# Attention in a decoder trunk: plain float32 matmuls for scores and for the products with V, in place of three products of split parts

## The chip, the cores and the metric

The kernel runs on one core of one Trainium2 chip. The metric is the device time of one execution in microseconds (us). Engines are named as the profile names them: PE is TensorE's matmul stream, PEld its weight loads, DVE is VectorE, ACT is ScalarE, SP issues the DMAs.

## What is computed

A decoder trunk of two layers on 256 tokens of width 1024, all in float32: a gated short convolution with a feed-forward block (ConvGLU), then attention with a feed-forward block, then a norm. With 256 tokens there is one block of keys, so the block selection falls away and the attention is plain causal attention of 16 heads of 64 columns, with a bias that depends on the distance. The part that the change touches, cut to what matters:

```python
sc = einsum("hqd,hkd->hqk", q, k) * scale + bias      # per head; causal, else -1e30
p  = softmax(sc)
o  = einsum("hqk,hkd->hqd", p, v)                      # 16 heads x 64 columns
return o.reshape(256, 1024) @ w_o
```

## The kernel before

**Split operands.** Nearly every matmul is made of three: an operand x is split into `hi` (x written as fp32r) and `lo` (x minus hi), and `mm3` (lines 160 to 163) adds hi x hi, hi x lo and lo x hi in PSUM. Weights arrive by DMA as `rawB` (8 KB in a partition) or `rawS` (4 KB), ACT writes `hiB`/`hiS` (line 86), DVE writes `loB`/`loS` (line 92). For activations `split_act` (lines 362 to 366) does the same with the tiles `sh` and `sl`. A few small matmuls take plain float32 operands and no split: the sums of squares (line 320), a broadcast of a row (line 334) and the table of biases (line 351).

**Attention.** Two heads make a pair j, eight pairs in all. `heads` sets PE's order: `v_step` makes V in four blocks of 256 columns (0, 1, 2, and block 3 after the last pair), `qk_step(j)` makes Q and K of pair j transposed (48 matmuls of 256 columns into the bank `qb[j]`), and behind each comes `attend(i)`, which puts on PE the transposes of pair i-2, the scores of pair i-1 and the products with V of pair i-3, in this order, and behind them the work of ACT and DVE that feeds later calls. So scores of a pair stand alone behind `qk_step(1)` and, with transposes ahead of them, behind `qk_step(2)`; six calls have transposes, scores and products together (behind `qk_step(3)` to `qk_step(7)` and behind V's block 3); two more calls, between the steps of the output product `wo`, have products and no scores (the first has transposes ahead of them).

**Scores** (line 623): in a pair, head e lies on partitions 64e to 64e+63 of the tiles `qh` and `ql`, so a matmul of one head has 64 rows. The queries of the second 128 tokens see 256 keys, those of the first see 128. For each of the two chunks there are three products, and in each the two heads stand next to each other.

**Products with V** (`pv`, lines 668 to 674): for each head, `mm3` runs with all 128 columns of V that belong to the pair as weights (`vh`, `vl`) and with the transposed probabilities (`sh`, `sl`) as moving operand, 256 columns and then 128; of the 128 partitions of the result half is used (`o_out`, lines 679 and 682).

**Banks.** PSUM tiles come from two rings, `acc` (4 banks) and `up` (3). In the attention, `qb`, V's block 3 and the products take `up` banks.

Of the kernel before, what the change touches and what calls it, by code (L numbers as in the profile page):

```python
# [11 lines left out]
F32 = mybir.dt.float32  # L12
F32R = mybir.dt.float32r
I32 = mybir.dt.int32
AF = mybir.ActivationFunctionType
OP = mybir.AluOpType

S = 256
D = 1024
KT = D // 128  # L20
# [17 lines left out]
def f32(ap):  # L38
    return ap.bitcast(F32)
# [3 lines left out]
def yoco_kernel(ctx: ExitStack, tc: tile.TileContext, t: dict, out: bass.AP):  # L43
    nc = tc.nc
    V, A, G, PE = nc.vector, nc.scalar, nc.gpsimd, nc.tensor

    const = ctx.enter_context(tc.tile_pool(name="const", bufs=1))
    wpool = ctx.enter_context(tc.tile_pool(name="wpool", bufs=1))
    act = ctx.enter_context(tc.tile_pool(name="act", bufs=2))
    tmp = ctx.enter_context(tc.tile_pool(name="tmp", bufs=2))  # L50
# [46 lines left out]
    def hi(tag, part=0, parts=1):  # L97

        n = ptr[tag][0]
        if n < len(by_tag[tag]) and (by_tag[tag][n].prev is None or by_tag[tag][n].prev.used):  # L100
            by_tag[tag][n].split_hi(part, parts)
            ptr[tag][0] += part == parts - 1

    def lo(tag, part=0, parts=1):

        n = ptr[tag][1]
        if n < len(by_tag[tag]) and by_tag[tag][n].hi is not None:
            by_tag[tag][n].split_lo(part, parts)
            if part == parts - 1:
                ptr[tag][1] += 1  # L110
                if n + RAW_BUFS[tag] < len(by_tag[tag]):
                    by_tag[tag][n + RAW_BUFS[tag]].load()
# [47 lines left out]
    def mm3(o, wh, wl, xh, xl, start, stop):  # L160
        PE.matmul(o, wh, xh, start=start, stop=False, skip_group_check=True)  # L161
        PE.matmul(o, wh, xl, start=False, stop=False, skip_group_check=True)  # L162
        PE.matmul(o, wl, xh, start=False, stop=stop, skip_group_check=True)  # L163
# [74 lines left out]
    def shifted(pool, name, tag, rows, **kw):  # L238

        t = pool.tile([128, rows * S + 64], F32R, name=name, tag=tag, **kw)  # L240
        return t[:, 48:48 + rows * S].rearrange("p (k s) -> p k s", s=S)
# [14 lines left out]
    def parts_tiles(moved=False):  # L256
        return Rows("xh", moved), Rows("xl", moved)
# [58 lines left out]
    def rstd_cols(sq):  # L316

        ps = psum.tile([128, 512], F32, name="misc", bufs=1)
        for c in range(2):
            PE.matmul(ps[:, c:c + 1], sq[:, 2, c * 128:(c + 1) * 128], ones[:, 0:1],  # L320
                      start=(c == 0), stop=True, skip_group_check=True)
        w = tmp.tile([128, 8], F32, name="nw")
        ms, y, a = w[:, 0:2], w[:, 2:4], w[:, 4:6]
        V.tensor_scalar(ms, ps[:, 0:2], 1.0 / D, EPS, op0=OP.mult, op1=OP.add)
        rsqrt(ms, y, a)
        dg = tmp.tile([128, 2, 128], F32, name="dg", tag="bias")
        for c in range(2):
            V.tensor_scalar(dg[:, c, :], ident, y[:, c:c + 1], None, op0=OP.mult)
        return y, dg

    def rstd_rows(dg, scales=(1.0,), orders=(same,)):

        ps = psum.tile([128, 512], F32, name="misc", bufs=1)
        PE.matmul(ps[:, :S], ones, dg.rearrange("p c s -> p (c s)"), start=True, stop=True)
        r = act.tile([128, 2, S], F32, name="rr", bufs=1)
        for n, s in enumerate(scales):
            A.activation(r[:, n, :], orders[n](ps[:, :S]), AF.Copy, scale=s)
        return r
# [23 lines left out]
    def split_act(src, n):  # L362

        h, lw = (tmp.tile([128, 384 + 64], F32R, name="s" + x, tag="z" + x, bufs=4)[:, 16:16 + n]
                 for x in "hl")
        return (h, lw), lambda: A.activation(h, src, AF.Copy), lambda: V.tensor_sub(lw, src, f32(h))  # L366
# [28 lines left out]
    rr = None  # L395
# [39 lines left out]
    rr = rstd_rows(dg)  # L435
# [125 lines left out]
    hot = bias_load()  # L561
    xvh, xvl, sq = boundary(acc, xT, P_KVN, rev)
    xqh, xql = parts_tiles()
    vh = wpool.tile([128, 2, D], F32R, name="vh", tag="hiB2")
    vl = wpool.tile([128, 2, D], F32R, name="vl", tag="loB2")
    oh = None
    ol = shifted(act, "ol", "ol", KT, bufs=1)
    vb, qb, qs, sb, pr, pt, ps_, ob, bias = {}, {}, {}, {}, {}, {}, {}, {}, {}
    ycol = rr = None
# [15 lines left out]

    def v_out(n):
        cols = slice(n * 256, (n + 1) * 256)
        for c in range(2):
            A.activation(vh[:, c, cols], vb[n][:, c, :], AF.Identity, scale=ycol[:, c:c + 1])
        for c in range(2):  # L590
            V.scalar_tensor_tensor(vl[:, c, cols], vb[n][:, c, :], ycol[:, c:c + 1], f32(vh[:, c, cols]),
                                   op0=OP.mult, op1=OP.subtract)

    def qk_step(j, ks=range(KT)):
        u = WH["q", j]
# [7 lines left out]
        u.used = ks[-1] == KT - 1  # L603

    def qk_out(j):
        q = tmp.tile([128, 2, S], F32, name="u", bufs=2)
        V.tensor_mul(q, qb[j], rr)
        h = tmp.tile([128, 2, S], F32R, name="qh", tag="cv", bufs=2)
        lw = tmp.tile([128, 2, S], F32R, name="ql", tag="ql", bufs=2)
        A.activation(h, q, AF.Copy)  # L610
        qs[j] = h, lw
        return lambda: V.tensor_sub(lw, q, f32(h))

    def scores(j, bank):
        h, lw = qs[j]
        for e in range(2):
            sb[j, e] = bank()
        for c, cols in ((1, slice(0, 256)), (0, slice(256, 384))):
            tok, ks = slice(c * 128, (c + 1) * 128), slice(128 - c * 128, S)
            for n, (q, k) in enumerate(((h, h), (h, lw), (lw, h))):  # L620
                for e in range(2):
                    d = slice(e * 64, (e + 1) * 64)
                    PE.matmul(sb[j, e].rearrange("p a s -> p (a s)")[:, cols], q[d, 0, tok], k[d, 1, ks],  # L623
                              start=(c == 1 and n == 0), stop=(n == 2), skip_group_check=True)

    CHUNKS = ((0, slice(0, 256), slice(0, 256)), (1, slice(256, 384), slice(0, 128)))

# [22 lines left out]
    def transposes(j, bank):  # L650
        for e in range(2):
            pt[j, e] = bank()
            b = pt[j, e].rearrange("p a s -> p (a s)")
            p = pr[j, e]
            PE.transpose(b[:, 0:128], p[:, 256:384], ident)
            PE.transpose(b[:, 128:256], p[:, 128:256], ident)
            PE.transpose(b[:, 256:384], p[:, 0:128], ident)

    def pt_out(j):
        low = []  # L660
        for e in range(2):
            b = pt[j, e].rearrange("p a s -> p (a s)")[:, 0:384]
            ps_[j, e], make_hi, make_lo = split_act(b, 384)
            make_hi()
            low.append(make_lo)
        return lambda: [f() for f in low]

    def pv(j, bank):
        b = ob[j] = bank()
        f = slice(j * 128, (j + 1) * 128)  # L670
        for e in range(2):
            h, lw = ps_[j, e]
            mm3(b[:, e, :], vh[:, 1, f], vl[:, 1, f], h[:, 0:256], lw[:, 0:256], start=(e == 0), stop=False)
            mm3(b[:, e, 128:256], vh[:, 0, f], vl[:, 0, f], h[:, 256:384], lw[:, 256:384], start=False, stop=True)

    def o_out(j):
        for e in range(2):
            d = slice(e * 64, (e + 1) * 64)
            A.activation(oh[d, j, :], ob[j][d, e, :], AF.Copy)
        for e in range(2):  # L680
            d = slice(e * 64, (e + 1) * 64)
            V.tensor_sub(ol[d, j, :], ob[j][d, e, :], f32(oh[d, j, :]))

    class Held:

        used = False

    next(u for u in UP[1] if u.slot == 2).prev = Held
    low_q, low_p, fin = {}, {}, {}

    def attend(i, qk=True, s=True, tr=True, v=True, banks=(acc_bank, acc_bank, up_bank)):

        if tr and 0 <= i - 2 < KT:
            transposes(i - 2, banks[0])
        if s and 0 <= i - 1 < KT:
            scores(i - 1, banks[1])
        if v and 0 <= i - 3 < KT:
            pv(i - 3, banks[2])
        if qk:
            hi("B")  # L700
        if qk and i < KT:
            low_q[i] = qk_out(i)
        if tr and 0 <= i - 2 < KT:
            low_p[i - 2] = pt_out(i - 2)
        if s and 0 <= i - 1 < KT:
            fin[i - 1], inverse = softmax(i - 1)
        if qk:
            lo("B")
        if s and 0 <= i - 1 < KT:
            inverse()  # L710
        if tr and 0 <= i - 2 < KT:
            low_p[i - 2]()
        if qk and i < KT:
            low_q[i]()
        if v and 0 <= i - 3 < KT:
            o_out(i - 3)
        if s and 0 <= i - 1 < KT:
            fin[i - 1]()

    for kind, n in heads:  # L720
        if kind == "v":
            vb[n] = acc_bank() if n < 3 else up_bank()
            if n == 1:
                v_step(1, range(0, 4))
                bias_table(hot)
                ycol, dg = rstd_cols(sq)
                v_step(1, range(4, 8))
                oh = shifted(act, "oh", "oh", KT, bufs=1)
            elif n == 2:
                v_step(2, range(0, 2))  # L730
                rr = rstd_rows(dg, (-0.125, 1.0), (rev, same))
# [185 lines left out]
```

## Time and profile before

| | |
|---|---|
| median of 3 runs | 583.97 us (583.82 to 584.67) |
| profiled execution, its own time | 584.08 us |
| its span (first to last instruction) | 582.1 us |
| PE busy | 573.4 us (98%), 4745 matmuls |
| DVE busy, ACT busy | 460.9 us (79%), 359.7 us (62%) |
| chain of waits that ends last | PE 97% |

The profile is of one execution; 2.0 us of its time lie outside the span. A busy PE row means that matmuls were in flight; how fast they follow each other is read from the starts of neighbouring rows, since a matmul's own duration includes its way through the array.

### The profile page before, as it was taken

The page shows a single profiled execution, that of the slowest core. Times are in us where ns is not written, and L with a number is a line of the kernel's source. Part 1 is how long each engine was busy: PE and PEld are TensorE (multiplying, and loading weights), DVE is VectorE, ACT ScalarE, POOL GpSimd, SP SyncE. Part 2 cuts the span into 40 slices and gives each one's busy share as a digit, 9 for nine tenths or more (in the row PEclk, how much of TensorE's full clock was granted, in tenths as well). Part 3 has the DMA queues.
Part 4 walks back from the last instruction along what each step waited for, and adds up shares of the span by engine and source line. Part 5 has one row for each costly group of instructions (what it writes and reads, how often), then busy time and mean ns, then how long its engine had stood idle before and what let it go on. Part 6 is the DMA issues. An engine that isn't in the chain of part 4 may idle for free.

```text
span 582.1 us, 11537 instructions
## 1 busy us (share of the span) xinstructions
PE 573.4 (98%) x4745; PEld 558.4 (96%) x4745; DVE 460.9 (79%) x781; ACT 359.7 (62%) x570; POOL 3.6 (1%) x15
## 2 busy tenths in 40 slices
PE   8999999999999999999999999999999999999995
PEld 8999999999999999999999999999999999999994
DVE  5899769888778777877977887757997787777865
ACT  7765347566566555665758997748675566556443
POOL 0000000000000000000000000000000000000001
PEclk9999999999999999999999999999999999999999
DMA  8985673545554566544446564434655644553111
GB/s 290 404 285 195 214 256 114 212 147 217 217 187 166 191 217 213 173 167 175 147 171 220 181 243 165 145 110 146 218 180 218 216 169 169 207 216 117 65 37 73
DMA packets 24236, 108.51 MB, mean 186 GB/s; under 512 B 2759, under 2 KB 5496, under 8 KB 16248
## 3 DMA queue, kind: packets, MB, share of 16 engines
q1 hardware_dynamic: 23864, 107.46, 52.1%
q8 instruction: 37, 0.61, 0.4%
q10 hardware_dynamic: 320, 0.32, 0.2%
q14 instruction: 15, 0.12, 0.1%
HBM read 106.70 MB, written 1.07 MB: 185 GB/s over the span
## 4 chain that ended last, share of the span: by engine, by line
PE 97%; DMA 1%; ACT 1%; DVE 0%; issue 0%; SPq 0%; POOLq 0%; POOL 0%; DVEq 0%; ACTq 0%
PE up L161 20%; PE up L163 20%; PE up L162 20%; PE acc L161 7%; PE acc L163 7%; PE acc L162 6%; PE acc L189 3%; PE acc L188 3%; PE acc L187 3%; PE acc L623 1%; PE acc L579 1%; PE acc L581 1%; PE acc L582 1%; DMA xres<-xT 1%; PE up L582 0%; PE up L579 0%
## 5 line engine op out<-in xcount | busy, mean ns | idle before, releaser
L161 PE MATMUL up<-xh,hiB 128*128 128x256 f32 x944 | 263.2, 279 | 0.3 <-ACT hiB L86 0.3
L163 PE MATMUL up<-xh,loB 128*128 128x256 f32 x944 | 261.5, 277 | 0.2 <-DVE loB L92 0.2
L162 PE MATMUL up<-xl,hiB 128*128 128x256 f32 x944 | 261.7, 277 | 0.0
L161 PEld LDWEIGHTS up<-xh,hiB 128*128 128x128 f32 x944 | 177.5, 188 | 1.6 <-ACT hiB L86 0.6
L162 PEld LDWEIGHTS up<-xl,hiB 128*128 128x128 f32 x944 | 177.5, 188 | 0.8
L163 PEld LDWEIGHTS up<-xh,loB 128*128 128x128 f32 x944 | 177.4, 188 | 0.7 <-DVE loB L92 0.7
L92 DVE TENSOR_TENSOR loB<-rawB,hiB 128x2048 fp32r<-128x2048 f32 (+2 forms) x75 | 147.6, 1973 | 3.9 <-ACT hiB L86 3.9
L86 ACT ACTIVATE hiB<-rawB 128x2048 fp32r<-128x2048 f32 (+1 forms) x73 | 123.6, 1697 | 17.2 <-PE acc L582 6.0
L92 DVE TENSOR_TENSOR loS<-rawS,hiS 128x1024 fp32r<-128x1024 f32 (+2 forms) x73 | 83.7, 1148 | 13.8 <-ACT hiS L86 13.5
L498 ACT ACTIVATE cv<-u,pk 128x256 f32<-128x256 f32 x88 | 48.2, 595 | 72.8 <-DVE u L491 72.8
L369 DVE SCALAR_TENSOR_TENSOR cv<-u,pk,cv 128x255 f32<-128x255 f32 x192 | 81.4, 479 | 2.7 <-ACT cv L498 1.7
L86 ACT ACTIVATE hiS<-rawS 128x1024 fp32r<-128x1024 f32 (+1 forms) x71 | 71.6, 1010 | 9.7 <-PE acc L162 6.0
L491 DVE TENSOR_TENSOR u<-up,rr 128x512 f32<-128x512 f32 x44 | 30.3, 689 | 58.7 <-PE up L163 57.3
L161 PE MATMUL acc<-sh,hiS 128*128 128x256 f32 x240 | 66.3, 276 | 0.0
L163 PE MATMUL acc<-sh,loS 128*128 128x256 f32 x240 | 66.3, 276 | 0.0
L162 PE MATMUL acc<-sl,hiS 128*128 128x256 f32 x240 | 66.3, 276 | 0.0
L366 ACT ACTIVATE sh<-hid 128x256 fp32r<-128x256 f32 x52 | 21.7, 416 | 59.7 <-DVE hid L512 55.0
L163 PEld LDWEIGHTS acc<-sh,loS 128*128 128x128 f32 x240 | 45.1, 188 | 0.0
L161 PEld LDWEIGHTS acc<-sh,hiS 128*128 128x128 f32 x240 | 45.1, 188 | 0.0
L162 PEld LDWEIGHTS acc<-sl,hiS 128*128 128x128 f32 x240 | 45.1, 188 | 0.0
L189 PE MATMUL acc<-hiS,sl 128*128 128x512 f32 (+1 forms) x89 | 34.8, 391 | 0.0
L188 PE MATMUL acc<-loS,sh 128*128 128x512 f32 (+1 forms) x89 | 34.6, 389 | 0.0
(157 smaller groups left out, 756.9 us busy)
## 6 DMA issues: line engine op xcount, KB each, us to landing
rawB<-w_up SPq DMA_DIRECT2D x44, 1024.0 KB, 4.8
rawS<-w_dn SPq DMA_DIRECT2D x44, 512.0 KB, 3.4
rawB<-w_qk SPq DMA_DIRECT2D x8, 1024.0 KB, 4.9
rawB<-w_mc SPq DMA_DIRECT2D x6, 1024.0 KB, 7.7
rawS<-w_mo SPq DMA_DIRECT2D x8, 512.0 KB, 3.3
rawB<-w_v SPq DMA_DIRECT2D x4, 1024.0 KB, 4.8
rawS<-w_o SPq DMA_DIRECT2D x8, 512.0 KB, 3.5
rawS<-w_mb SPq DMA_DIRECT2D x7, 512.0 KB, 5.6
```

The costliest lines, as they stand in the source:

```text
L86: A.activation(self.hi[:, c], self.raw[:, c], AF.Copy)
L92: V.tensor_sub(self.lo[:, c], self.raw[:, c], f32(self.hi[:, c]))
L161: PE.matmul(o, wh, xh, start=start, stop=False, skip_group_check=True)
L162: PE.matmul(o, wh, xl, start=False, stop=False, skip_group_check=True)
L163: PE.matmul(o, wl, xh, start=False, stop=stop, skip_group_check=True)
L187: PE.matmul(o, hh[:, tok], u.hi[:, f], start=first, stop=False, skip_group_check=True)
L188: PE.matmul(o, hh[:, tok], u.lo[:, f], start=False, stop=False, skip_group_check=True)
L189: PE.matmul(o, hl[:, tok], u.hi[:, f], start=False, stop=last, skip_group_check=True)
L366: return (h, lw), lambda: A.activation(h, src, AF.Copy), lambda: V.tensor_sub(lw, src, f32(h))
L369: V.scalar_tensor_tensor(o[:, back:], u[:, :S - back], w, o[:, back:], op0=OP.mult, op1=OP.add)
L491: V.tensor_mul(u, ub[j], rr[:, 0:1, :].to_broadcast([128, 2, S]))
L498: A.activation(o[:, half, :], u[:, half, :], AF.Identity, scale=cw[half][2], bias=par(P_FCB, c0 + half * FJ))
```

## The change

The scores and the products with V take plain float32 operands. `qh`, `ql`, `vh`, `vl`, `sh` and `sl` of the attention go; instead there are `u` (Q and K of a pair, as DVE writes them from the bank), `vs` (V scaled, chunk 0 by ACT and chunk 1 by DVE) and `pT` (the transposed probabilities, head 0 copied by ACT and head 1 by DVE). A chunk of scores is one matmul in place of three. In the products each head has only its own 64 columns of V as weights and writes partitions 64e to 64e+63 of one half of the bank, so that `o_out` takes one instruction on each of ACT and DVE in place of two. The diff, without the lines of `attend` that only drop the calls of the removed `lo` parts:

```diff
@@ -561,8 +561,7 @@
     hot = bias_load()
     xvh, xvl, sq = boundary(acc, xT, P_KVN, rev)
     xqh, xql = parts_tiles()
-    vh = wpool.tile([128, 2, D], F32R, name="vh", tag="hiB2")
-    vl = wpool.tile([128, 2, D], F32R, name="vl", tag="loB2")
+    vs = wpool.tile([128, 2, D], F32, name="vs", tag="hiB2")
     oh = None
     ol = shifted(act, "ol", "ol", KT, bufs=1)
     vb, qb, qs, sb, pr, pt, ps_, ob, bias = {}, {}, {}, {}, {}, {}, {}, {}, {}
@@ -585,11 +584,8 @@
 
     def v_out(n):
         cols = slice(n * 256, (n + 1) * 256)
-        for c in range(2):
-            A.activation(vh[:, c, cols], vb[n][:, c, :], AF.Identity, scale=ycol[:, c:c + 1])
-        for c in range(2):
-            V.scalar_tensor_tensor(vl[:, c, cols], vb[n][:, c, :], ycol[:, c:c + 1], f32(vh[:, c, cols]),
-                                   op0=OP.mult, op1=OP.subtract)
+        A.activation(vs[:, 0, cols], vb[n][:, 0, :], AF.Identity, scale=ycol[:, 0:1])
+        V.tensor_scalar(vs[:, 1, cols], vb[n][:, 1, :], ycol[:, 1:2], None, op0=OP.mult)
 
     def qk_step(j, ks=range(KT)):
         u = WH["q", j]
@@ -603,25 +599,19 @@
         u.used = ks[-1] == KT - 1
 
     def qk_out(j):
-        q = tmp.tile([128, 2, S], F32, name="u", bufs=2)
-        V.tensor_mul(q, qb[j], rr)
-        h = tmp.tile([128, 2, S], F32R, name="qh", tag="cv", bufs=2)
-        lw = tmp.tile([128, 2, S], F32R, name="ql", tag="ql", bufs=2)
-        A.activation(h, q, AF.Copy)
-        qs[j] = h, lw
-        return lambda: V.tensor_sub(lw, q, f32(h))
+        qs[j] = tmp.tile([128, 2, S], F32, name="u", bufs=2)
+        V.tensor_mul(qs[j], qb[j], rr)
 
     def scores(j, bank):
-        h, lw = qs[j]
+
         for e in range(2):
             sb[j, e] = bank()
         for c, cols in ((1, slice(0, 256)), (0, slice(256, 384))):
             tok, ks = slice(c * 128, (c + 1) * 128), slice(128 - c * 128, S)
-            for n, (q, k) in enumerate(((h, h), (h, lw), (lw, h))):
-                for e in range(2):
-                    d = slice(e * 64, (e + 1) * 64)
-                    PE.matmul(sb[j, e].rearrange("p a s -> p (a s)")[:, cols], q[d, 0, tok], k[d, 1, ks],
-                              start=(c == 1 and n == 0), stop=(n == 2), skip_group_check=True)
+            for e in range(2):
+                d = slice(e * 64, (e + 1) * 64)
+                PE.matmul(sb[j, e].rearrange("p a s -> p (a s)")[:, cols], qs[j][d, 0, tok], qs[j][d, 1, ks],
+                          start=(c == 1), stop=True, skip_group_check=True)
 
     CHUNKS = ((0, slice(0, 256), slice(0, 256)), (1, slice(256, 384), slice(0, 128)))
 
@@ -657,36 +647,33 @@
             PE.transpose(b[:, 256:384], p[:, 0:128], ident)
 
     def pt_out(j):
-        low = []
         for e in range(2):
             b = pt[j, e].rearrange("p a s -> p (a s)")[:, 0:384]
-            ps_[j, e], make_hi, make_lo = split_act(b, 384)
-            make_hi()
-            low.append(make_lo)
-        return lambda: [f() for f in low]
+            ps_[j, e] = tmp.tile([128, 384], F32, name="pT", tag="zh", bufs=4)
+            if e:
+                V.tensor_copy(ps_[j, e], b)
+            else:
+                A.activation(ps_[j, e], b, AF.Copy)
 
     def pv(j, bank):
+
         b = ob[j] = bank()
-        f = slice(j * 128, (j + 1) * 128)
-        for e in range(2):
-            h, lw = ps_[j, e]
-            mm3(b[:, e, :], vh[:, 1, f], vl[:, 1, f], h[:, 0:256], lw[:, 0:256], start=(e == 0), stop=False)
-            mm3(b[:, e, 128:256], vh[:, 0, f], vl[:, 0, f], h[:, 256:384], lw[:, 256:384], start=False, stop=True)
+        for c, q, cols in ((1, slice(0, 256), slice(0, 256)), (0, slice(128, 256), slice(256, 384))):
+            for e in range(2):
+                f = slice(j * 128 + e * 64, j * 128 + e * 64 + 64)
+                PE.matmul(b[e * 64:e * 64 + 64, 0, q], vs[:, c, f], ps_[j, e][:, cols],
+                          start=(c == 1), stop=(c == 0), skip_group_check=True)
 
     def o_out(j):
-        for e in range(2):
-            d = slice(e * 64, (e + 1) * 64)
-            A.activation(oh[d, j, :], ob[j][d, e, :], AF.Copy)
-        for e in range(2):
-            d = slice(e * 64, (e + 1) * 64)
-            V.tensor_sub(ol[d, j, :], ob[j][d, e, :], f32(oh[d, j, :]))
+        A.activation(oh[:, j, :], ob[j][:, 0, :], AF.Copy)
+        V.tensor_sub(ol[:, j, :], ob[j][:, 0, :], f32(oh[:, j, :]))
 
     class Held:
 
         used = False
 
     next(u for u in UP[1] if u.slot == 2).prev = Held
-    low_q, low_p, fin = {}, {}, {}
+    fin = {}
 
     def attend(i, qk=True, s=True, tr=True, v=True, banks=(acc_bank, acc_bank, up_bank)):
 
...
```

What stands on PE in a call of `attend` with all three parts (the first one, behind `qk_step(3)`). `qh` and `ql` are the split Q and K, `sh`/`sl` the split probabilities, `vh`/`vl` the split V; "x2" is the two heads. Before, the scores and head 0's half of the products:

```order
L657 MATMUL acc<-ident,pr 128x128
L623 MATMUL acc<-qh 128x256 x2
L623 MATMUL acc<-ql,qh 128x256 x2
L623 MATMUL acc<-qh,ql 128x256 x2
L623 MATMUL acc<-qh 128x128 x2
L623 MATMUL acc<-ql,qh 128x128 x2
L623 MATMUL acc<-qh,ql 128x128 x2
L161 MATMUL up<-sh,vh 128x256
L162 MATMUL up<-sl,vh 128x256
L163 MATMUL up<-sh,vl 128x256
L161 MATMUL up<-sh,vh 128x128
L162 MATMUL up<-sl,vh 128x128
```

and now, from the last transpose to the first matmul of the next `qk_step`:

```order
L647 MATMUL acc<-ident,pr 128x128
L613 MATMUL acc<-u 128x256 x2
L613 MATMUL acc<-u 128x128 x2
L664 MATMUL up<-pT,vs 64x256 x2
L664 MATMUL up<-pT,vs 64x128 x2
L161 MATMUL up<-xh,hiB_4028 128x256
```

24 matmuls (12 of scores and 12 of products) have become 8, at the same place between the transposes and the next step; each of the 8 is a plain float32 matmul, and a product's result has 64 partitions.

What stands on DVE behind V's block 3 (`v_out(3)`, line 591 before and 588 now), between the reciprocals of one softmax and the first read of the next scores. Before:

```order
L648 RECIPROCAL st<-st 128x2 x2
L366 TENSOR_TENSOR sl<-acc,sh 128x384 x2
L612 TENSOR_TENSOR ql<-u,qh 128x512
L682 TENSOR_TENSOR ol<-up,oh 64x256 x2
L591 SCALAR_TENSOR_TENSOR vl<-up,nw,vh 128x256 x2
L635 ISA sc,st<-acc,bias 128x256
```

and now:

```order
L638 RECIPROCAL st<-st 128x2 x2
L669 TENSOR_TENSOR ol<-up,oh 128x256
L588 TENSOR_SCALAR vs<-up,nw 128x256
L654 COPY pT<-up 128x384
L625 ISA sc,st<-acc,bias 128x256
```

`v_out` reads the bank on DVE once and no longer needs `vh` from ACT first; the copy of head 1's probabilities has moved ahead of the reads of the scores.

## Rows read from the trace of the kernel before

**Rows 1.** The page: span, busy time of each engine with its share of the span, and the chain of waits that ended last, by engine.

```profile
span 582.1 us, 11537 instructions
PE 573.4 (98%) x4745; PEld 558.4 (96%) x4745; DVE 460.9 (79%) x781; ACT 359.7 (62%) x570; POOL 3.6 (1%) x15
...
PE 97%; DMA 1%; ACT 1%; DVE 0%; issue 0%; SPq 0%; POOLq 0%; POOL 0%; DVEq 0%; ACTq 0%
```

**Rows 2.** Busy time of each engine (number of its instructions) in three stretches of the attention: the calls with scores and no products, the five calls with scores and products behind `qk_step(3)` to `qk_step(7)`, and the end with the first steps of `wo`; then PE's clock as a share of its higher level, DMA share and GB/s. The columns are PE, PEld, DVE, ACT and POOL.

```profile
305.30:320.00 14.70, 14.70 (x133) 14.20 (x133) 11.12 (x29) 12.80 (x31) 0.00 (x0) 1.00 0.61 217
320.00:362.00 42.00, 42.00 (x385) 40.97 (x385) 35.95 (x88) 38.03 (x93) 0.00 (x0) 1.00 0.58 199
362.00:381.00 19.00, 18.65 (x168) 18.34 (x168) 12.83 (x26) 13.79 (x29) 0.00 (x0) 1.00 0.47 152
```

**Rows 3.** Who waited for whom on PE between 280 and 400 us: us in total, times, the longest.

```profile
PE up L161 <- DVE vl L591: 0.3, 1, 0.3
```

**Rows 4.** PE's instructions in order of time in the call of `attend` behind `qk_step(4)`: start us, us, engine, line, operation, out<-in, rows*columns of weights, partitions x columns that move, how many in the row. L623 is the scores (first and last of six rows), L161 with `sh` and `vh` the first matmul of the products, with `xh` that of the next `qk_step`.

```profile
328.52 0.39 PE L623 MATMUL acc<-qh 64*128 64x256 f32 x2
...
329.15 0.28 PE L623 MATMUL acc<-qh,ql 64*128 64x128 f32 x2
329.35 0.39 PE L161 MATMUL up<-sh,vh 128*128 128x256 f32 x1
...
330.78 0.33 PE L161 MATMUL up<-xh,hiB 128*128 128x256 f32 x1
```

**Rows 5.** The weight loads of the same call, columns as above: the last transpose (L657), the first two and the last of the scores, the first of the products, the first of the next `qk_step`.

```profile
328.21 0.14 PEld L657 LDWEIGHTS acc<-ident,pr 128*128 128x128 f32 x1
328.52 0.19 PEld L623 LDWEIGHTS acc<-qh 64*128 64x128 f32 x2 [0.17 <-issue]
328.62 0.19 PEld L623 LDWEIGHTS acc<-ql,qh 64*128 64x128 f32 x2
...
329.09 0.19 PEld L623 LDWEIGHTS acc<-qh,ql 64*128 64x128 f32 x2
329.35 0.19 PEld L161 LDWEIGHTS up<-sh,vh 128*128 128x128 f32 x1
...
330.72 0.19 PEld L161 LDWEIGHTS up<-xh,hiB 128*128 128x128 f32 x1
```

**Rows 6.** Plain float32 matmuls in the V steps (line 351: 384 columns; line 334: 256 columns; each is one matmul of the program and two of the trace), with their neighbours, from the timeline of PE.

```profile
283.88 0.81 PE L351 MATMUL up<-hot,rb 33*16 33x384 f32 x2
...
289.14 0.28 PE L582 MATMUL acc<-hiB,xl 128*128 128x256 f32 x1
289.26 0.59 PE L334 MATMUL misc<-dg,ones 128*128 128x256 f32 x2
289.50 0.47 PE L579 MATMUL acc<-hiB,xh 128*128 128x256 f32 x1
289.81 0.28 PE L581 MATMUL acc<-loB,xh 128*128 128x256 f32 x1
```

**Rows 7.** The weight loads of line 320 (two plain float32 matmuls of 128 columns of weights and a single moving column, four loads in the trace) and the next load behind them.

```profile
284.62 0.52 PEld L320 LDWEIGHTS misc<-ones,sq 128*128 128x128 f32 x4 [0.64 <-issue]
285.06 0.19 PEld L579 LDWEIGHTS acc<-hiB,xh 128*128 128x128 f32 x1
```

**Rows 8.** Weight loads around the scores behind `qk_step(1)`, which stand alone: the first of the scores, the first of `qk_step(2)`.

```profile
305.32 0.19 PEld L623 LDWEIGHTS acc<-qh 64*128 64x128 f32 x2
...
306.15 0.19 PEld L161 LDWEIGHTS up<-xh,hiB 128*128 128x128 f32 x1
```

**Rows 9.** Weight loads around products without scores, behind `wo(1)`: the last transpose, the first product, the first load of `wo(2)`.

```profile
371.45 0.14 PEld L657 LDWEIGHTS up<-ident,pr 128*128 128x128 f32 x1
371.56 0.19 PEld L161 LDWEIGHTS up<-sh,vh 128*128 128x128 f32 x1
...
372.94 0.19 PEld L161 LDWEIGHTS acc<-oh,hiS 128*128 128x128 f32 x1
```

**Rows 10.** PE, ACT and DVE behind V's block 3, from the timeline; in brackets the idle time before a row and what ended it.

```profile
363.44 0.28 PE L623 MATMUL acc<-qh,ql 64*128 64x128 f32 x2
364.07 0.39 PE L161 MATMUL up<-sh,vh 128*128 128x256 f32 x1 [0.35 <-DVE vl L591]
...
362.27 0.84 ACT L589 ACTIVATE vh<-up,nw 128x256 fp32r<-128x256 f32 x2 [1.58 <-PE up L582]
...
363.14 0.88 DVE L591 SCALAR_TENSOR_TENSOR vl<-up,nw,vh 128x256 fp32r<-128x256 f32 x2 [2.16 <-ACT vh L589]
```

**Rows 11.** The third and the 48th (last) matmul of `qk_step(2)`, which follows scores alone, and of `qk_step(4)`, which follows products.

```profile
306.49 0.28 PE L163 MATMUL up<-xh,loB 128*128 128x256 f32 x1
...
311.79 0.28 PE L163 MATMUL up<-xh,loB 128*128 128x256 f32 x1
...
322.56 0.28 PE L163 MATMUL up<-xh,loB 128*128 128x256 f32 x1
...
327.65 0.28 PE L163 MATMUL up<-xh,loB 128*128 128x256 f32 x1
```

**Rows 12.** Groups of DVE and ACT instructions between 305 and 382 us: line, engine, operation, out<-in, shapes, count | busy us, mean ns of one | idle before.

```profile
L366 DVE TENSOR_TENSOR sl<-acc,sh 128x384 fp32r<-128x384 f32 x12 | 6.0, 542 | 0.0
L612 DVE TENSOR_TENSOR ql<-u,qh 128x512 fp32r<-128x512 f32 x7 | 4.8, 680 | 0.0
...
L610 ACT ACTIVATE qh<-u 128x512 fp32r<-128x512 f32 x7 | 4.3, 613 | 0.0
```

More of the change, by code (lines that the diff above doesn't have):

```diff
@@ L701, in attend @@
         if qk and i < KT:
-            low_q[i] = qk_out(i)
+            qk_out(i)
         if tr and 0 <= i - 2 < KT:
-            low_p[i - 2] = pt_out(i - 2)
+            pt_out(i - 2)
         if s and 0 <= i - 1 < KT:
@@ L710, in attend @@
             inverse()
[L711 to L714, printed above, removed]
         if v and 0 <= i - 3 < KT:
```

## The prediction

> **What bounds the kernel now.** I read the page first. PE is busy for 98% of the span and the chain that ended last is PE for 97% of it [rows 1], so the kernel is as long as PE's queue. Then the stretches of the attention: PE has no hole in the first two, ACT is busy for 38.03 of 42.00 us and DVE for 35.95 [rows 2]. That is close to full, so the list of waits comes next: PE waited for another engine once between 280 and 400 us, 0.3 us [rows 3]. Work taken from ACT and DVE therefore buys nothing beyond that one wait, and the question is how long PE takes for scores and products. [...]
>
> **What a plain float32 matmul costs.** Line 334 is one: it starts at 289.26, and one ordinary matmul after it the next starts at 289.81 [rows 6]. From 0.55 us I take 0.12 for that ordinary one (289.14 to 289.26) and keep 0.43 us for 256 columns, two passes of 0.215. Line 351 bears it out: its two passes last 0.81 us together; an ordinary matmul of 256 columns lasts 0.28 and is followed after 0.11, so 0.17 is the way through the array, and 0.64 is left for twice 384 columns: 0.83 ns a column against 0.84. So 128 columns take two passes of 0.107. A load of 128 columns of weights takes 0.11 (four in 0.44, [rows 7]) and fits beneath either pass. One head's chunk pair of 256 and 128 columns then costs 0.43 + 0.21 = 0.64 us. Split, it costs six passes of 0.11 to 0.12, about 0.68: in bare streaming hardly anything is gained, and everything hangs on how the two heads overlap.
>
> **How the heads overlap.** In the scores before, the heads lie on different rows of the array and stand next to each other, and the trace has the two under one start: twelve matmuls, 0.63 us between the first and last start [rows 4]. Now each head's two passes stand in a row: 0a 0b 1a 1b. Pass 0b has to wait for 0a, which has the same rows; 1a stands behind 0b. If 1a can't pass it, 1a runs beside 0b and 1b beside the next chunk's first pass. The second head then starts 0.21 late and needs its own 0.64: 0.21 + 0.64 = 0.85 us for a pair's scores. If 1a passed it, both heads would run together from the start, 0.64. If nothing overlapped, 1.28. No row shows a matmul passing one that waits, and I take 0.85. For the products no row shows two matmuls on different columns of the array; the nearest is the scores on different rows, so 0.85 again, bounds 0.64 and 1.28.
> [...]
>
> **Price of changing the shape of the array.** From the last transpose's load to the first load of the scores it is 0.31 us (328.21 to 328.52) where loads otherwise follow in 0.11: 0.20 lost. Leaving the scores: the last load at 329.09 is in at 329.20, 128 columns end by 329.26, and the next load comes at 329.35, 0.09 later [rows 5]. Products before changed no shape; now they are entered and left with a change.
>
> **The sum, from load to load.** Scores: 0.83 before (328.52 to 329.35 [rows 5], 0.83 also when alone [rows 8]); now 0.11 for the first load + 0.85 + 0.09 = 1.05. Products: 1.37 before (329.35 to 330.72, [rows 5]), 1.38 without scores [rows 9]; now a load of half the columns, which I put at 0.055 with 0.11 as its bound, + 0.85 + 0.09 = 1.00. Where products follow other matmuls directly, entering adds 0.20.
> - Six calls with both: 1.05 + 1.00 - 2.20 = -0.15 each, -0.90.
> - Two calls with scores and no products: 1.05 - 0.83 = +0.22 each, +0.44.
> - Two calls with products and no scores: 1.00 + 0.20 - 1.38 = -0.18 each, -0.36.
> - The one wait. Behind V's block 3 the first product starts 0.63 after the last score (363.44 to 364.07, [rows 10]), elsewhere 0.20 (329.15 to 329.35, [rows 4]): 0.43 lost. The product wants the `up` bank of V's block 3, and that is free only when ACT has read it twice and then DVE twice. Now ACT and DVE read it once each, side by side: from 362.27, one instruction is 0.42 on ACT and at most 0.48 on DVE [rows 10], done by 362.8, about a microsecond before the product. -0.43.
> Together -1.25.
> - The pace behind it. `qk_step(2)`, entered with a change of shape, takes 45 steps in 5.30 us, 0.118 each; `qk_step(4)`, entered from products without one, takes them in 5.09, 0.113 [rows 11]. I can't name the cause. From now on `qk_step(4)` to `qk_step(7)` are entered with a change too. Bounds: 0, or 4 x 0.21 = +0.84, and as much again if the steps of `wo` behind the last products slow down as well. I take +0.84, since both steps that are entered so today are slow.
>
> The sum is -0.41. The profiled execution took 584.08 us, 0.11 above the median of 583.97; 584.08 - 0.41 = 583.67, and on the median's level **583.6 us**. Differences under 0.2%, 1.2 us, can't be told from no change here.
>
> **What costs nothing.** A call loses the halves `ql` (0.68) and one `sl` (0.54) on DVE and `qh` (0.61) on ACT [rows 12], among others; it gains a copy of 128x384 on DVE, as long as the `sl` that it replaces. That hides behind PE's 8.5 us from call to call (42.00 us for about five calls, [rows 2]). The copies of the probabilities are needed one call later, so they would have to slip by several microseconds to be late; were one late, PE would wait by that slip in each of eight calls. With less to do both engines only run ahead further.
>
> **Rivals.**
> 1. The heads overlap fully, 0.64 in place of 0.85 in sixteen places: -3.4, so 580.2 with the slow pace and 579.3 without. For it: the scores before do start in pairs. Against: their matmuls stood in alternating order. 12%.
> 2. As forecast, but the slow pace doesn't come: -1.25, 582.7, a hair beyond the 0.2%. For it: `qk_step(4)` is made of the same matmuls as `qk_step(2)` and keeps the quicker pace [rows 11], so the slow one isn't their own. 22%.
> 3. The load for head 1 doesn't overtake head 0's waiting pass and starts only with it. Each change of head then waits for a load: +0.21 in the scores (two loads of 0.11) and +0.06 in the products (half the columns, one of the two hidden), +0.27 a pair, +2.1: 585.7, 584.9 without the slow pace. Rows 5 speak against it (loads of both heads appear under one start), but there heads alternate. 12%.
> 4. Slower: column halves of the array don't overlap, since the moving operands of both heads need all 128 rows. The products then take 1.28, +0.43 in eight calls: +3.4, 587.0 (586.2 without the slow pace). It decides as soon as the second head's first pass starts only behind the first head's last. Nothing in the trace excludes it. 12%.
> 5. Neither overlaps: +6.8, 590.4. Against it stand the paired starts of the scores. 8%.
>
> [...]
>
> **How the numbers follow.** The forecast with the slow pace has 32%, the rivals 66%, and 2% are for something else. Its own range is 582.6 to 584.5, from no slow pace to a slow `wo`. The whole range goes from rival 1 without slow pace to rival 4 with it, 579.2 to 587.1; it leaves out rival 5 and the rest. Faster by over 0.2%: rival 1 and some three quarters of rival 2, 0.29. Slower by over 0.2% (from 585.2): rivals 4 and 5 and half of rival 3, 0.26. Within: 0.45.
>
> **What would show it.** In the changed kernel's timeline: eight plain passes of scores in a call, the second head's first start 0.21 behind the first head's, 0.85 from the first pass to the end of the last, and about 1.05 from the scores' first load to the products'. The same for the products; a second head that starts 0.43 late shows rival 4, equal starts rival 1. The wait behind V's block 3 gone. The steps of `qk_step(4)` at 0.118 or 0.113. I am wrong if a plain pass with half the rows or columns has another price than line 334's, if going from halves of rows to halves of columns costs more than 0.2, or if PE starts to wait for `pT`.

## The result, and the profile after

The changed kernel takes 579.98 us (median of 4 runs, 579.40 to 580.10) against 584.26 (583.82 to 584.67) for the kernel before in the same runs: a ratio of 0.9928, with an interval of 0.9916 to 0.9941, faster by 4.3 us. It lies inside the range, and 3.6 us below the forecast of 583.6. The profiled execution took 579.40 us.

The page after, the rows that answer to [rows 1]:

```profile
span 577.6 us, 11330 instructions
PE 569.1 (99%) x4681; PEld 550.6 (95%) x4681; DVE 446.7 (77%) x753; ACT 347.5 (60%) x542; POOL 3.6 (1%) x15
...
PE 97%; DMA 1%; ACT 1%; DVE 0%; SPq 0%; issue 0%; POOLq 0%; POOL 0%; DVEq 0%; ACTq 0%
```

PE is as full as before and its busy time is 4.3 us shorter, which is the whole gain: 64 matmuls fewer in the trace, eight fewer for each pair of heads (the 24 of a pair became 8, which the trace shows as 16). DVE and ACT lost 14.2 and 12.2 us; no more can have come of that than the one wait behind V's block 3, 0.4 us.

Two stretches of the attention (columns PE, PEld, DVE, ACT, POOL, then clock, DMA share, GB/s). The first is cut at the same events as the first of [rows 2]; the second runs on to the end of the products behind V's block 3, so it holds six calls with scores and products and the five steps between them:

```profile
304.90:319.43 14.53, 14.53 (x126) 13.86 (x125) 9.54 (x26) 11.37 (x28) 0.00 (x0) 1.00 0.60 215
319.43:361.10 41.67, 41.67 (x367) 37.95 (x366) 29.41 (x80) 33.70 (x81) 0.00 (x0) 1.00 0.61 208
```

The second of these in the kernel before, up to the same event:

```profile
320.00:365.50 45.50, 45.15 (x415) 43.81 (x415) 38.30 (x99) 41.26 (x98) 0.00 (x0) 1.00 0.55 190
```

It is 3.83 us shorter now. The clock is at 1.00 as before. The list of what PE waited for between 280 and 400 us is now empty.

The weight loads of the call behind `qk_step(4)`, as in [rows 5]:

```profile
327.08 0.14 PEld L647 LDWEIGHTS acc<-ident,pr 128*128 128x128 f32 x1
327.39 0.73 PEld L613 LDWEIGHTS acc<-u 64*128 64x128 f32 x8 [0.17 <-issue]
328.24 0.63 PEld L664 LDWEIGHTS up<-pT,vs 128*64 128x64 f32 x8
329.05 0.19 PEld L161 LDWEIGHTS up<-xh,hiB 128*128 128x128 f32 x1 [0.17 <-DVE st L625]
```

From load to load the scores take 0.85 us (0.83 before), the products 0.81 (1.37 before). The forecast had 1.05 and 1.00. Where the two heads stand is seen by cutting each of the two groups at its starts; a row gives the length of the window and, in brackets, how many matmuls and loads were in flight in it. First the scores (line 613 alone):

```profile
327.38:327.70 0.32, 0.31 (x2) 0.30 (x4) 1.00 1.03 435
327.70:327.92 0.22, 0.22 (x4) 0.19 (x2) 1.00 1.05 447
327.92:328.03 0.11, 0.11 (x4) 0.10 (x2) 1.00 0.21 65
```

And the products of the same call (line 664 alone):

```profile
328.24:328.50 0.26, 0.26 (x2) 0.20 (x4) 1.00 1.08 386
328.50:328.72 0.22, 0.22 (x4) 0.14 (x2) 1.00 0.96 335
328.72:328.83 0.11, 0.11 (x4) 0.10 (x2) 1.00 2.16 298
```

In the first window of each group there are two matmuls: one pass of each head, though head 0's second pass stands between them in the program. (The rows don't name the heads; but eight passes are through in the time of four, and a head's own passes share their rows or columns.) In the next there are four, two that drain and two that have started. The first windows are longer, 0.32 and 0.26, since the first load lies open there: a head's second load starts 0.11 and 0.06 behind its first. The other windows last 0.22 for 256 columns and 0.11 for 128: the price of a plain pass was right, and the heads overlap wholly, 0.64 and not 0.85 for a pair.

### The profile page after: what moved, and what is told of

It is laid out like the page before. It is cut to its first block, busy times and chain, and to the rows that moved or that the text cites. A ratio compares the mean times of both kernels' runs of the same rounds, so it can differ in the third digit from the quotient of the medians.

```text
span 577.6 us, 11330 instructions
## 1 busy us (share of the span) xinstructions
PE 569.1 (99%) x4681; PEld 550.6 (95%) x4681; DVE 446.7 (77%) x753; ACT 347.5 (60%) x542; POOL 3.6 (1%) x15
## 4 chain that ended last, share of the span: by engine, by line
PE 97%; DMA 1%; ACT 1%; DVE 0%; SPq 0%; issue 0%; POOLq 0%; POOL 0%; DVEq 0%; ACTq 0%
PE up L161 20%; PE up L162 19%; PE up L163 19%; PE acc L161 7%; PE acc L162 7%; PE acc L163 7%; PE acc L189 3%; PE acc L188 3%; PE acc L187 3%; PE acc L613 1%; PE up L664 1%; PE acc L578 1%; PE acc L581 1%; PE acc L580 1%; DMA xres<-xT 1%; PE up L578 0%
## 5 line engine op out<-in xcount | busy, mean ns | idle before, releaser
L161 PE MATMUL up<-xh,hiB 128*128 128x256 f32 x944 | 263.3, 279 | 0.2
L161 PEld LDWEIGHTS up<-xh,hiB 128*128 128x128 f32 x944 | 177.4, 188 | 2.3 <-ACT hiB L86 0.6
L161 PE MATMUL acc<-sh,hiS 128*128 128x256 f32 x240 | 66.3, 276 | 0.0
L161 PEld LDWEIGHTS acc<-sh,hiS 128*128 128x128 f32 x240 | 45.0, 188 | 0.0
```

## The experiments

**Which part gives the gain.** Two kernels make one half of the change each. The scores alone:

```diff
...
-            for n, (q, k) in enumerate(((h, h), (h, lw), (lw, h))):
-                for e in range(2):
...
+            for e in range(2):
...
+                          start=(c == 1), stop=True, skip_group_check=True)
...
```

> The kernel before with the scores alone as plain float32; the products with V stay split and on all 128 columns. Theory A (the gain is that the two heads' products run beside each other on halves of the columns; plain float32 by itself gains nothing): a pair's scores take 0.85 us from their first weight load to the next one in place of 0.83, so eight of them cost +0.2, with the pace of the steps behind them open by some 0.4 either way: 583.8 to 584.8 against 584.1 to 584.3. Rival B (plain float32 relieves ACT and DVE and PE runs quicker by it, about half of the gain each for scores and products): 582 or less.

Measured: 583.87 us against 584.13, ratio 0.9999 (0.9990 to 1.0008). Its weight loads in the same call:

```profile
327.74 0.73 PEld L617 LDWEIGHTS acc<-u 64*128 64x128 f32 x8 [0.17 <-issue]
328.59 0.19 PEld L161 LDWEIGHTS up<-sh,vh 128*128 128x128 f32 x1
...
329.96 0.19 PEld L161 LDWEIGHTS up<-xh,hiB 128*128 128x128 f32 x1
```

0.85 for the scores and 1.37 for the products. Plain scores gain nothing, and with 4.1 us less work for ACT and 4.9 for DVE over the whole span PE runs no quicker. PE's wait behind V's block 3 is still in this trace.

The products alone (scores split again, the diff above turned round in the changed kernel):

> The changed kernel with the scores put back to split parts; the products with V are plain and on halves of the columns. Theory A: all of the gain is here, 0.80 us a pair from load to load in place of 1.37, six times -0.57, twice -0.38 where the products are entered with a change of shape that was not there, and the wait behind V's block 3 gone (-0.43): 579.6 to 580.4. Rival B: about 582.

Measured: 579.95 us, ratio 0.9928 (0.9915 to 0.9940), the ratio of the whole change. In this trace too the scores take 0.83 to 0.84 and the products 0.80. PE's wait behind V's block 3 is gone. Theory A holds: all of the gain is in the products and in the plain V that they read.

**Plain float32 or halves of the columns.** The changed kernel with the products over all 128 columns again:

```diff
-        for c, q, cols in ((1, slice(0, 256), slice(0, 256)), (0, slice(128, 256), slice(256, 384))):
-            for e in range(2):
-                f = slice(j * 128 + e * 64, j * 128 + e * 64 + 64)
-                PE.matmul(b[e * 64:e * 64 + 64, 0, q], vs[:, c, f], ps_[j, e][:, cols],
+        f = slice(j * 128, (j + 1) * 128)
+        for e in range(2):
+            PE.matmul(b[:, e, :], vs[:, 1, f], ps_[j, e][:, 0:256], start=(e == 0), stop=False, skip_group_check=True)
+            PE.matmul(b[:, e, 128:256], vs[:, 0, f], ps_[j, e][:, 256:384], start=False, stop=True,
...
```

(`o_out` takes its four instructions again.)

> The changed kernel with each head's products again on all 128 columns of V, so that both heads use the whole array one after the other, still plain float32. Theory A: four matmuls in a row, 0.43 + 0.21 for each head, 1.28 to 1.3 us a pair against 1.37 split and 0.80 in halves; eight times -0.07 to -0.09, the wait behind block 3 gone (-0.43), scores +0.2: 583.0 to 583.8. Rival B: as quick as the changed kernel within 1 us, 579.5 to 581.

Measured: 583.07 us, ratio 0.9981 (0.9972 to 0.9990). The loads of its products:

```profile
330.06 0.30 PEld L663 LDWEIGHTS up<-pT,vs 128*128 128x128 f32 x2
330.38 0.41 PEld L664 LDWEIGHTS up<-pT,vs 128*128 128x128 f32 x2
...
331.36 0.19 PEld L161 LDWEIGHTS up<-xh,hiB 128*128 128x128 f32 x1
```

1.30 us a pair, about what four plain matmuls one after the other come to (twice 0.43 + 0.21, 1.28). Of the 0.57 that a pair gains, plain float32 gives 0.07 and the halves of the columns 0.50. That is also rival 4 of the prediction measured by itself: had the column halves not overlapped, this is what the products would cost. They do overlap. No run has split products on halves of the columns. Split scores, on halves of the rows, take 0.83 us a pair where plain ones take 0.85, so the 0.50 may not need plain operands; that is not shown.

**Does a matmul pass one that waits?** The changed kernel with the order turned, so that all of head 0's passes stand ahead of head 1's:

```diff
-        for c, cols in ((1, slice(0, 256)), (0, slice(256, 384))):
-            tok, ks = slice(c * 128, (c + 1) * 128), slice(128 - c * 128, S)
-            for e in range(2):
-                d = slice(e * 64, (e + 1) * 64)
+        for e in range(2):
+            d = slice(e * 64, (e + 1) * 64)
+            for c, cols in ((1, slice(0, 256)), (0, slice(256, 384))):
+                tok, ks = slice(c * 128, (c + 1) * 128), slice(128 - c * 128, S)
...
```

and the same in `pv`.

> The changed kernel with the order of scores and products turned: both chunks of head 0, then both of head 1, the same matmuls. Theory C (PE takes any matmul whose part of the array is free, however many of the other head's wait ahead of it): nothing changes, the heads still start together, 580 within 0.6. Rival D (a matmul passes at most the one that waits directly ahead of it, the second pass of the head's neighbour): the second head starts 0.53 us behind the first, +0.53 in sixteen places, 588 to 589. Rival E (no passing at all; the starts in pairs come from an order of passes that is already alternating in the program as loaded): the second head starts only with the first head's last pass, +0.53 likewise.

Measured: 580.16 us, ratio 0.9930 (0.9917 to 0.9944). Again two matmuls in the first window of the scores, and four in the next:

```profile
327.20:327.52 0.32, 0.31 (x2) 0.31 (x4) 1.00 0.97 410
327.52:327.74 0.22, 0.22 (x4) 0.20 (x2) 1.00 0.88 372
```

Head 1's first pass starts 0.01 us behind head 0's first, although three passes of head 0 with their loads wait ahead of it. Theory C holds at this distance, and D and E of the expectation fall.

Whether only plain float32 does this was asked of the kernel before, whose split matmuls are of one pass each:

```diff
-            for n, (q, k) in enumerate(((h, h), (h, lw), (lw, h))):
-                for e in range(2):
-                    d = slice(e * 64, (e + 1) * 64)
+            for e in range(2):
+                d = slice(e * 64, (e + 1) * 64)
+                for n, (q, k) in enumerate(((h, h), (h, lw), (lw, h))):
...
```

> The kernel before with the scores' order turned inside a chunk: three products of head 0, then three of head 1. Theory C (a matmul whose rows of the array are free starts, whatever waits ahead of it): 0.83 us from the scores' first load to the next one as before, heads starting within 0.02 of each other, the time unchanged. If only two-pass matmuls did this: head 1 starts about 0.33 behind head 0 in each chunk and a pair's scores take 1.2 to 1.5, 587 to 589.

Measured in one run: 583.88 us, 583.91 for the kernel before. Its loads:

```profile
328.17 0.19 PEld L623 LDWEIGHTS acc<-qh 64*128 64x128 f32 x2 [0.17 <-issue]
...
329.01 0.19 PEld L161 LDWEIGHTS up<-sh,vh 128*128 128x128 f32 x1
```

0.84 with both heads in every row: head 1 had two waiting matmuls ahead of it and passed them. So in this run split matmuls of one pass each did it as well.

That the order on PE is the one written is an inference from the traces: the gap between the two heads' first starts grows with what stands between them. It is 3 to 4 ns with nothing (split scores of the kernel before), 6 to 8 ns with one pass (scores and products of the changed kernel), 10 ns with two (this run), 12 to 14 ns with three (head 0 first), in every pair of each trace. Had the order been an alternating one as loaded (rival E), the gap would have no reason to grow.

**How far.** Head 0's two products ten times over, ahead of head 1's two:

```diff
...
+        for e in range(2):
+            f = slice(j * 128 + e * 64, j * 128 + e * 64 + 64)
+            for again in range(1 if e else 10):
+                for c, q, cols in ((1, slice(0, 256), slice(0, 256)), (0, slice(128, 256), slice(256, 384))):
...
```

> The changed kernel with head 0's two products of a pair written ten times over (each time overwriting, so the result stays) before head 1's two stand in the program: 20 plain matmuls, 40 passes and 40 loads wait ahead of head 1. It shows how far ahead PE looks. Without a limit: head 1 starts within 0.02 us of head 0. With a limit of n instructions, head 1 starts when all but about n of the 80 have gone: at some 0.08 us an instruction, 32 instructions would be a start about 3.9 us late, 64 about 1.3 us late. The whole takes about 5.8 us longer for each pair, 626 us.

Measured in one run: 627.74 us. The 44 passes of the first pair, in two windows:

```profile
320.88:326.78 5.90, 5.89 (x36) 4.48 (x37) 1.00 0.38 112
326.78:327.58 0.80, 0.80 (x10) 0.59 (x8) 1.00 1.07 451
```

For 5.90 us head 0 runs alone, 36 passes. Then eight are left (two of the ten in the second row are still draining): the last four of head 0 and the four of head 1, in pairs. So head 1 starts together with head 0's 37th pass, with three waiting ahead of it, the 38th to the 40th; it is the 37th in all eight pairs. In the programs so far a matmul passed one, two and three waiting matmuls with their loads; with 40 passes of the other head ahead, it had to wait until 36 of them were done. None of the limits named in the expectation fits: I had put it at 32 or 64 instructions or none, and it is six to eight (three passes with their loads, and the one that has just started). This was seen on halves of the columns and with plain float32 alone. What sets it is not shown.

**The pace behind a change of shape.** One matmul of 256 columns cut in two, in four stretches of the changed kernel:

```diff
+        if cut[0]:
+            for c in (slice(0, 128), slice(128, 256)):
+                PE.matmul(o[:, c], wl, xh[:, c], start=False, stop=stop, skip_group_check=True)
+            cut[0] = False
...
+            cut[0] = j in (0, 3) and k == 4
...
```

> The changed kernel with one matmul of 256 columns cut into two of 128 in each of four stretches that run at 0.118 us a step (the steps of pair 0, pair 3, V's block 3 and the output product behind the last products). If the slow pace is a phase between loads and matmuls that a disturbance can end, the steps behind the cut take 0.113 in some of the four; gain 0.1 for half a step, 0.4 for the output product, together up to 1.0 us less 0.2 for the cuts. If the pace belongs to the operands of these steps, nothing changes behind the cuts: the time is the changed kernel's plus 0.2.

Measured in one run: 579.84 us. PE in `qk_step(0)`, around the cut (L167):

```profile
295.06 0.28 PE L163 MATMUL up<-xh,hiB 128*128 128x256 f32 x1
...
297.29 0.28 PE L164 MATMUL up<-xl,hiB 128*128 128x256 f32 x1
297.41 0.34 PE L167 MATMUL up<-xh,loB 128*128 128x128 f32 x2
297.58 0.33 PE L163 MATMUL up<-xh,hiB 128*128 128x256 f32 x1
...
298.11 0.28 PE L164 MATMUL up<-xl,hiB 128*128 128x256 f32 x1
...
302.99 0.28 PE L170 MATMUL up<-xh,loB 128*128 128x256 f32 x1
```

Ahead of the cut 19 steps take 2.23 us, 0.117 each; from the fifth step behind it 43 take 4.88, 0.113 each, with the same operands. The cuts in the steps of pair 3 and of V's block 3, at 0.118 in the changed kernel, did the same; the output product behind the last products already ran at the quick pace in this trace, and the 48 matmuls of `wo` ahead of them, quick in the changed kernel, ran at 0.118. In the traces of the kernel before and of the changed one no stretch of one kind of step between 285 and 395 us changes its pace once its first dozen steps are past. So here the operands don't fix the pace: steps of the same kind took 0.117 ahead of the cut and 0.113 behind it. The cut cost about 0.11 us (0.70 from 297.41 to 298.11, where five steps at 0.117 take 0.59), so half a `qk_step` at the quick pace gains no more than it pays. The time of one run can't show this.

**The last two pairs together.** The products of pairs 6 and 7 together, at the later of their two places:

```diff
-    attend(KT + 1, banks=(up_bank, None, up_bank))
+    attend(KT + 1, v=False, banks=(up_bank, None, up_bank))
...
-    attend(KT + 2, banks=(None, None, up_bank))
+    for j in (KT - 2, KT - 1):
+        pv(j, up_bank)
+    for j in (KT - 2, KT - 1):
+        o_out(j)
```

> The changed kernel with the products of pairs 6 and 7 put together at the later of their two places, so that the array changes its shape twice less. A change on entering costs 0.20 and one on leaving 0.09 plus a load of 0.05 to 0.11 that lies open: 0.3 to 0.4 less than the changed kernel, 579.6, if nothing waits for the later output of pair 6; the pace of the steps behind can move it by 0.4 either way.

Measured: 579.11 us (578.48 to 579.23), ratio to the kernel before 0.9914 (0.9901 to 0.9928), with all five runs below all four of the changed kernel. The intervals of the two ratios overlap (the changed kernel's is 0.9916 to 0.9941), and the two were not run side by side: against the kernel before in its own runs the one saves 4.8 us and the other 4.3, so of the 0.9 us between the medians 0.5 can be counted on. The joined products:

```profile
373.24 1.28 PEld L664 LDWEIGHTS up<-pT,vs 128*64 128x64 f32 x16
374.69 0.19 PEld L161 LDWEIGHTS acc<-oh,hiS 128*128 128x128 f32 x1 [0.17 <-issue]
```

1.45 us for two pairs in place of 0.80 twice, and one entry of 0.20 less: 0.35, as expected. The pace gives another 0.4: the 96 matmuls of the output product behind the last products take 10.90 us here and 11.30 in the changed kernel, the step after it is quicker by 0.17, and the 48 matmuls between the two places are slower by 0.20. From the transposes of the last pair to the second layer the two traces differ by 0.73 us in all.

The same with a cut right behind the broadcast of the row in V's block 2:

```diff
...
+                for f in (slice(0, 128), slice(128, 256)) if n == 2 and k == 2 and c == 0 else (slice(0, 256),):
+                    PE.matmul(o[:, f], xvl[:, k, tok], wh[:, k, 0, f], start=False, stop=(k == KT - 1),
...
```

> The kernel with the products of pairs 6 and 7 joined, and one matmul of V's block 2, right behind the broadcast of the row, cut into two of 128 columns. If a cut ends the slow pace, the 130 steps from there to the first scores take 0.113 in place of 0.118: 0.57 us less 0.11 for the cut, 578.6 us against 579.1. If the slow pace comes back at once: 579.2.

Measured: 579.27 us (578.55 to 579.58), ratio 0.9914 (0.9900 to 0.9927), no gain. In its trace the steps behind the cut take 0.113 for 3.6 us, to the end of `v_step(2)`, and from the first steps of `qk_step(0)` on 0.118 again. The cut earned 0.14 and cost 0.11; with the next kind of step the slow pace was back.

## Why the prediction was right and where it was wrong

The range held and the verdict of the likeliest case, within 0.2% of no change, did not: it was rival 1, for which the prediction had 12%: 580.2 us with the slow pace and 579.3 without. That the range held is owed to this rival and not to the sum, which took a gain of 0.4 us and was 3.6 us off.

**The step that failed** is "How the heads overlap". It argued from 0a 0b 1a 1b that 1a can't pass 0b while 0b waits, and so put 0.85 us on a pair's scores and again on its products. Measured are 0.64 for both (two passes of 0.22 and two of 0.11 from the first start, the heads 0.01 apart). That is 0.21 us in sixteen places, the 3.4 us of rival 1. The prediction took "no row shows a matmul passing one that waits" for evidence that none does; but in the kernel before the heads alternated, so no row could have shown it. No run shows a pair's passes in 0.85 from the first start: turned orders with two and three waiting matmuls between the heads ran with starts 10 to 14 ns apart.

**The terms of the sum**, by the traces of the two kernels from load to load:

| term | forecast | measured |
|---|---|---|
| scores of a pair | 0.83 to 1.05 | 0.83 to 0.85 |
| products of a pair | 1.37 to 1.00 | 1.37 to 0.80 |
| eight pairs, both | -1.2 | -4.4 |
| entering the products directly, two places | +0.40 | +0.4 |
| the wait behind V's block 3 | -0.43 | -0.42 |
| pace of the steps | +0.84 | +0.4 |
| sum (terms rounded) | -0.41 | -4.0 |

The last row can be compared with the stretch itself: from the first load of the V steps to the first of the second layer's steps behind the turn of the tokens it took 122.37 us before and 118.30 after, -4.07. The profiled spans differ by 4.5; the other 0.4 lie ahead of the V steps, where the programs are alike and where their start moves between 274.9 and 276.4 us from one trace to the next.

**What held.** PE alone bounds this kernel (97% of the chain that ended last, in the page after too), and relief of ACT and DVE bought nothing beyond the one wait (the kernel with plain scores, 583.87 against 584.13). A plain matmul took two passes of 0.84 ns a column (0.22 for 256, 0.11 for 128), and in bare streaming hardly anything was gained over three split ones (the products over all columns, 1.30 against 1.37). Going from the whole array into halves cost 0.20 (0.31 from 327.08 to 327.39, where loads otherwise follow in 0.11), and 0.1 passed behind the last pass before the next load (the last pass of the scores starts at 328.04 and takes 0.11, the next load comes at 328.24). The wait behind V's block 3 is gone. The slow term that the forecast put on four steps did not come as told: `qk_step(4)` to `qk_step(7)` keep 0.113 though entered with a change, `qk_step(2)` became quicker by 0.19, and instead the output product behind the last products and one step after it became slower by 0.4 and 0.17. Two stretches [rows 11] were too few for a rule, and the trace of the kernel before had one that speaks against it: V's block 3 comes directly behind split products, with no change of shape, and its third and 48th matmul are 45 steps of 0.118 apart.

```profile
356.65 0.28 PE L582 MATMUL up<-hiB,xl 128*128 128x256 f32 x1
...
361.95 0.28 PE L582 MATMUL up<-hiB,xl 128*128 128x256 f32 x1
```

So the +0.84 was put on the wrong places, and that its sign came out is luck.

**Rivals.** Rival 3 (loads that don't overtake) falls with the paired starts; rivals 4 and 5 fall with the products in halves, which take 0.80 where the same work over the whole array takes 1.30.

## What to carry to other kernels

If a matmul fills only half of the array, try another independent one on the other half: on halves of the columns that was worth 0.50 us of every 1.30 here, and the switch from split to plain operands 0.07. On halves of the rows the scores overlapped before and after, 0.83 and 0.85 from load to load. The order of the two hardly mattered with few matmuls between them (ratio 0.9930 with head 0 first, 0.9928 with the heads alternating; three waiting ones were passed, more in no run). So count what each part of the array has to do, and measure what going into halves and back adds: here about 0.3 us (0.20 and 0.1; 0.35 was saved by doing it once less). When a trace doesn't show a behaviour, ask whether its program could have shown it before taking that for evidence.

## What was not expected of the hardware

In these runs PE started a matmul on one half of the array ahead of waiting ones, with their loads, on the other half: ahead of three passes of plain float32, on halves of the rows and of the columns (first starts 12 to 14 ns apart, head 0 first), and ahead of two split matmuls of one pass each, on halves of the rows (10 ns). With 40 passes ahead, on halves of the columns, it started with the 37th of them, 5.90 us late.

The stream of 256-column matmuls ran at two paces, 0.113 and 0.118 us a step, over dozens of steps with the same operands and the clock at 1.00 (45 steps of `qk_step(2)` in 5.30 us before; 43 behind the cut of `qk_step(0)` in 4.88). A single cut matmul was followed by the quick pace in place of the slow one (0.117 to 0.113), and with a change from one kind of step to another the slow one was back (0.113 to 0.118, the joined products with a cut). What makes the two is open.
